# Delta rule's triangular matrices and their 32-block inverses issued beside the HGRN2 heads, and four PSUM banks for the levels

## The chip, the cores and the metric

One core of a Trainium2 chip runs one program: one layer of a diffusion backbone on 2048 latent and 128 context tokens. The metric is the device time of one execution in microseconds (us); the median of three runs counts. PE is TensorE (PEld its weight loads), DVE VectorE, ACT ScalarE, POOL GpSimd, SP the engine that issues this kernel's DMAs.

## The reference, cut to what matters

Two kinds of heads read one input projection. The first kind (HGRN2, "group A") is a gated linear recurrence over chunks of tokens, forward and backward. The second (gated DeltaNet, "group B") needs, per chunk, head and direction, the inverse of a unit lower triangular matrix that is made of keys and decays:

```
lower = where(strict, einsum('bhntk,bhnsk->bhnts', k_beta, k) * decay_mask, 0.0)
sol = triangular_solve(lower + eye(CHUNK), rhs, lower=True, unit_diagonal=True)
...
v_new = u_c - einsum('bhck,bhkv->bhcv', w_c, s)
o_c = einsum('bhtk,bhkv->bhtv', q_c, s) + einsum('bhts,bhsv->bhtv', attn_c, v_new)
s = s * d_c[..., None, None] + einsum('bhsk,bhsv->bhkv', kt_c, v_new)
```

The outputs of both kinds are normalised, gated, concatenated and projected; a SwiGLU feed-forward part follows.

## The kernel before

The kernel works on 17 chunks of 128 tokens (16 latent, one context), with 4 heads of each kind. Projections are cut into five pieces of 384 or 512 tokens; each piece is 24 matmuls (L257, tile `pj`, three PSUM banks), since weights and input are split in two parts for precision. In order:

- **Stage 1** (to about 494 us): norms, the delta rule's q, k, v columns and their convolution; the result goes to a DRAM scratch, `qkv_d`.
- **HGRN2 stage** (about 494 to 1040 us): per head a projection for q and one for v, then per direction one projection for the forget gate. The forget-gate pieces feed a chain: tanh and log on ACT (L488, L492), `th` on POOL (L494), a cumulative sum on DVE (L497 or L501), its middle subtracted on POOL (`G`, L508), two exponentials on ACT (L511, L512), two products on DVE (L515, L516), then small matmuls (L520 to L549). The state runs from chunk to chunk through three DVE operations, `T` (L547), `ns` (L552) and `ns` scaled (L553). "Gate half" below means the time of a head in which this chain runs; "value half" is the other, with the q and v projections.
- **Gate stage** (about 1040 to 1309 us): eight projections of output gates (`gate_block`, 960 matmuls on `pj`), and beside them the delta rule's matrices in three steps. `A1`, per chunk: keys loaded (`kTa`), four 128x128 products into a PSUM tile `pkk` (L592), decays per direction (`e`: a DMA broadcast, a mask on POOL at L599, an exponential on ACT at L602), the product of both on DVE (L604), a sum on POOL (L606) and a write to DRAM. `A2`, per batch of four chunks (one batch holds the context chunk alone): the 32x32 diagonal blocks come back into `A`, and a loop of 30 steps with two operations each (`pr`, L635, and `A`, L637) inverts them all at once. Three batches run on DVE, two on POOL. `A3`, per chunk ("levels"): 32-blocks are joined to 64 and 128 with small matmuls (tiles `pl` and `pn`, L675 to L701) and copies on ACT, POOL and DVE, from two PSUM banks and, for the later chunks, buffers that A1 no longer needs; the inverse goes to DRAM (`xt_d`).
- **Scan stage** (about 1309 to 1835 us): the delta rule's 16 steps in both directions, and the output projection's two halves as filler. Up to 1525 us the first half (`py`, L847) is under way; this is called the scan stage's first part.
- **Feed-forward stage** (from 1835 us).

Each engine takes its instructions in a fixed order, which a scheduler derives at build time from the order of the code, priorities and buffers; an instruction that waits holds everything behind it on its engine. All DMAs named here are issued by SP in one such order. `high_priority(1000)` lifts the A2 loops ahead of other work.

Of the kernel before, what the change touches and what calls it, by code (L numbers as in the profile page):

```python
# [24 lines left out]
H = 4  # L25
# [8 lines left out]
def hybrid_step(ctx: ExitStack, tc, x, vecs, ada1, ada2, bada, win, wgt, alog, dtb, sa, sb, wout, wg, wu, wd, normf,  # L34
# [37 lines left out]
    def tri(b, j, dims):  # L72
        return bass.AP(l_d[b].tensor, l_d[b].offset + j * 16 * BQ, dims)
# [64 lines left out]
        return (pl or gc).tile(shape, F32, tag=name, name=name)  # L138

    G, nG, eG, eL, ek, nrho, vbs, nrg = (K([P, 2, NT, H], n_) for n_ in "G nG eG eL ek nrho vbs nrg".split())  # L140
    gq = pool(sK, "gq", right=True)
    bp = pool(sB, "bp", right=True)
    gts = K([P, NT, 16], "gts", bp)
    pjp = pool(s1, "pjp", 3, PSUM, right=True)
# [293 lines left out]
                nc.vector.tensor_tensor(out=nrg[:, d], in0=nrho[:, d], in1=eG[:, d], op=ALU.mult)  # L438


    with ExitStack() as sA:
        ap_ = pool(sA, "ap", 1)
        smask = ap_.tile([P, 512], F32, tag="smask", name="smask")

        mki = []
# [10 lines left out]
        for h in range(H):  # L456
# [3 lines left out]
            for i, (c0, n) in enumerate(PIECES):  # L460
                pj = proj(w, i)
                th = ap_.tile([P, 512], F32, tag="th", name="th", bufs=2)
                nc.scalar.activation(out=th[:, :n * P], in_=pj, func=AF.Tanh, scale=0.5)
                nc.vector.scalar_tensor_tensor(out=q2[i], in0=th[:, :n * P], scalar=1.0, in1=pj, op0=ALU.add,  # L464
                                               op1=ALU.mult)
            w = load_w(win[12 + h])
            for i, (c0, n) in enumerate(PIECES):
                pj = proj(w, i)
                th = ap_.tile([P, 512], F32, tag="th", name="th", bufs=2)
                nc.scalar.activation(out=th[:, :n * P], in_=pj, func=AF.Copy)  # L470
                pt = ps1.tile([P, 4, P], F32, tag="tr", name="ptv", bufs=2)
                for j in range(n):
                    nc.tensor.transpose(pt[:, j, :], th[:, j * P:(j + 1) * P], ident)
                nc.scalar.activation(out=vt[i], in_=pt[:, :n], func=AF.Copy, scale=0.5)
            for d in range(2):
                col = d * H + h
                w = load_w(win[4 + 4 * d + h])
# [5 lines left out]
                for i in order:  # L483
# [75 lines left out]
                    else:  # L559
                        of = ap_.tile([P, 4, P], F32, tag="of", name="of", bufs=1)[:, :n]  # L560
                        dma(out=of, in_=oav[:, c0:c0 + n, h, :])
                        nc.vector.tensor_tensor(out=og, in0=po[:, :n], in1=of, op=ALU.add)
                    dma(out=oav[:, c0:c0 + n, h, :], in_=og)

    sp1.close()

    def bcast_G(t, d, c):
        dma(out=t.rearrange("p h t -> p (h t)"),
            in_=gr_d[d].rearrange("(c h) t -> c (h t)", h=H)[c:c + 1, :].broadcast_to([P, H * P]))

    def rep_h(m):
        return m.rearrange("p (a t) -> p a t", a=1).to_broadcast([P, H, P])

    s1b = ExitStack()
    count = [0, 0]
    psl = pool(s1b, "psl", 2, PSUM)
    psp = pool(s1b, "psp", 2, PSUM)


    with ExitStack() as sG:  # L580
        gp = pool(sG, "gp", right=True)

# [3 lines left out]
        def A1(c, b, j):

            kT = W([P, H, P], "kTa")
            dma(out=kT, in_=qkv_d[c, :, 0])
            pk = psp.tile([P, H, P], F32, tag="pre", name="pkk")  # L590
            for h in range(H):
                nc.tensor.matmul(out=pk[:, h], lhsT=kT[:, h], rhs=kT[:, h], start=True, stop=True)  # L592
            es = []
            for d in range(2):
                e = W([P, H, P], "e", 4)
                es.append(e)
                bcast_G(e, d, c)
                s = 1 if d == 0 else -1
                nc.gpsimd.affine_select(out=e, in_=e, pattern=[[0, H], [-s, P]], compare_op=ALU.is_gt, fill=1e30,  # L599
                                        base=0, channel_multiplier=s)  # L600
                for h in range(H):
                    nc.scalar.activation(out=e[:, h], in_=e[:, h], func=AF.Exp, scale=-1.0, bias=G[:, d, c, h:h + 1])  # L602
                for h in range(H):
                    nc.vector.scalar_tensor_tensor(out=e[:, h], in0=pk[:, h], scalar=nrho[:, d, c, h:h + 1],  # L604
                                                   in1=e[:, h], op0=ALU.mult, op1=ALU.mult)
            nc.gpsimd.tensor_tensor(out=es[0], in0=es[0], in1=es[1], op=ALU.add)  # L606
            dma(out=tri(b, j, [[P, P], [4 * BQ, H], [1, P]]), in_=es[0])

        def A2_load(b):

            nf = 16 * NB[b]
            pb = max(nf, 32)
            np_ = pb + nf
            A = W([P, 32, 32], "A", 2)
            B = W([P, 32, 32], "B")
            if nf < pb:
                nc.gpsimd.memset(A[0:pb], 0.0)
            for t, p0 in ((A, 0), (B, pb)):
                dma(out=t[p0:p0 + nf], in_=tri(b, 0, [[BQ, nf], [P, 32], [1, 32]]))
            nc.vector.tensor_copy(out=A[pb:np_], in_=B[pb:np_].rearrange("p a b -> p b a"))  # L620
            nc.gpsimd.affine_select(out=A[0:np_], in_=A[0:np_], pattern=[[1, 32], [-1, 32]], compare_op=ALU.is_gt,
                                    fill=0.0, base=0, channel_multiplier=0)
            nc.gpsimd.memset(A[0:np_].rearrange("p a b -> p (a b)")[:, 0:1024:33], 1.0)
            return A

        def A2(b, A, e=nc.vector):

            nf = 16 * NB[b]
            pb = max(nf, 32)
            np_ = pb + nf  # L630
            pr = W([P, 240], "pr")
            for r in range(1, 31):
                m = 31 - r
                pv = pr[0:np_, 0:m * r].rearrange("p (i c) -> p i c", c=r)
                e.tensor_tensor(out=pv, in0=A[0:np_, r + 1:, r:r + 1].to_broadcast([np_, m, r]),  # L635
                                in1=A[0:np_, r:r + 1, :r].to_broadcast([np_, m, r]), op=ALU.mult)
                e.tensor_tensor(out=A[0:np_, r + 1:, :r], in0=A[0:np_, r + 1:, :r], in1=pv, op=ALU.add)  # L637
            T = W([P, 32, 32], "B")
            e.tensor_copy(out=T[0:np_], in_=A[0:np_].rearrange("p a b -> p b a"))
            for d, p0 in ((0, 0), (1, pb)):  # L640
                for a in range(2):
                    dma(out=xi_d[b][:, a, d], in_=(A, T)[a ^ d][p0:p0 + nf].rearrange("p a b -> p (a b)"))


        XT = [W([P, 2, H, P], f"XT{i}") for i in range(2)]
        NS = [W([P, 2, H, 64], "NS")]
        for t in XT + NS:
            nc.gpsimd.memset(t, 0.0)

        def A3(c, b, j):  # L650

            n = count[0]
            count[0] += 1
            xt = XT[n % 2]
            second = n >= NB[1] and n % 2 == 1

            dd = W([P, 2, 2, H, 32], "e", 4) if second else W([P, 2, 2, H, 32], "dd", 2)
            dma(out=dd.rearrange("p a d h s -> p (a d h) s"),
                in_=xi_d[b][j].rearrange("a d (h q) (i s) -> (q i) (a d h) s", q=4, s=32))
            L = W([P, H, P], "e", 4) if second else W([P, H, P], "L", 2)  # L660
            dma(out=L, in_=tri(b, j, [[P, P], [4 * BQ, H], [1, P]]))
            if second and len(NS) < 2:
                NS.append(W([P, 2, H, 64], "kTa"))
                nc.gpsimd.memset(NS[1], 0.0)
            na, s6 = (NS[int(second)][:, i] for i in range(2))
            g = lambda q: slice(32 * q, 32 * q + 32)
            for q in range(4):
                nc.scalar.activation(out=xt[g(q), :, :, g(q)], in_=dd[g(q), 1], func=AF.Copy)
# [35 lines left out]
                nc.vector.tensor_copy(out=xt[f, d, :, s], in_=p6[f, 1])  # L704
            dma(out=xt_d[c], in_=xt)

        batches = [[NL], [0, 15, 1, 14], [2, 13, 3, 12], [4, 11, 5, 10], [6, 9, 7, 8]]
        order = (1, 2, 3, 4, 0)
        blocks = []
        def chain(t):  # L710
            with tc.high_priority(1000):
                A2(order[t], blocks[t], nc.gpsimd if t in (3, 4) else nc.vector)

        def levels(t):
            for j, c in enumerate(batches[order[t]]):
                A3(c, order[t], j)

        for t in range(5):
            for j, c in enumerate(batches[order[t]]):
                A1(c, order[t], j)  # L720
            blocks.append(A2_load(order[t]))
            if t:
                chain(t - 1)
            if t == 1:
                levels(0)
        chain(4)
        for t in range(1, 5):
            levels(t)
# [831 lines left out]
```

## Time and profile before

| | |
|---|---|
| median of 3 runs | 3355.38 us (3352.89 to 3359.86) |
| the profiled execution's own time | 3358.57 us |
| its span | 3356.9 us |
| PE busy | 3121.5 us, 93% |
| DVE busy | 2089.0 us, 62% |
| ACT busy | 1519.0 us, 45% |
| POOL busy | 1254.8 us, 37% |
| mean granted TensorE clock | 0.964 |

The span is the time from the first to the last instruction; the execution's own time lies 1.7 us above it. Busy time is the union of an engine's instructions. PE's busy share says that PE is rarely without an instruction, not that it runs at its peak: at the lower of its two clocks it is busy for longer with the same work. So a stage is read by three figures, its length, PE's busy time and the granted clock, and by who ended PE's waits in it.

### The profile page before, as it was taken

The numbers are of one execution on the slowest core, as the hardware profiler recorded it, in microseconds if no ns is written. First come the engines' busy times: TensorE is split into PE (matmuls) and PEld (weight loads), VectorE is DVE, ScalarE is ACT, GpSimd is POOL, SyncE is SP. The second block draws the span as 40 slices with busy tenths as digits, with TensorE's granted clock in tenths as the row PEclk, the third lists the DMA queues.
The fourth block names the chain that finished last, engine by engine and source line by source line (L and its number), as shares of the span: only waits on it lengthen the run. The fifth ranks groups of instructions, "written<-read, shape, count | busy, mean of one in ns | idle before, by whom it ended". The sixth has DMA issues, their size and how long they took to land. (4 is left out here: it accounts for less than half of the span.)

```text
span 3356.9 us, 51604 instructions
## 1 busy us (share of the span) xinstructions
PE 3121.5 (93%) x18550; PEld 2792.2 (83%) x18550; DVE 2089.0 (62%) x4016; ACT 1519.0 (45%) x3233; POOL 1254.8 (37%) x1228
## 2 busy tenths in 40 slices
PE   7899989999999799998897999999999999899998
PEld 4687779999998677877786888888899998799997
DVE  4667744474553764564666777778565677565667
ACT  6455435374464544663764555454422223422222
POOL 1100001021121337413566544554545553544446
PEclk8999999999999988999998999999999999999999
DMA  5235410111114667877784877898656766655564
GB/s 221 72 109 145 116 55 29 53 44 36 53 39 138 172 179 230 265 249 253 240 263 152 304 287 286 298 325 314 223 192 212 240 211 230 228 193 194 184 201 155
DMA packets 331009, 620.12 MB, mean 185 GB/s; under 512 B 77818, under 2 KB 177954, under 8 KB 324354
## 3 DMA queue, kind: packets, MB, share of 16 engines
q1 hardware_dynamic: 330754, 616.83, 56.0%
q8 instruction: 147, 2.41, 0.3%
q14 instruction: 108, 0.88, 0.1%
HBM read 435.22 MB, written 181.51 MB: 184 GB/s over the span
## 5 line engine op out<-in xcount | busy, mean ns | idle before, releaser
L257 PE MATMUL pj<-hh,wh 128*128 128x384 f32 (+2 forms) x1480 | 546.0, 369 | 12.9 <-DVE q L464 6.6
L257 PE MATMUL pj<-hl,wh 128*128 128x384 f32 (+2 forms) x1480 | 545.2, 368 | 0.3 <-POOL hl L231 0.3
L257 PE MATMUL pj<-hh,wl 128*128 128x384 f32 (+2 forms) x1480 | 545.3, 369 | 0.0
L257 PEld LDWEIGHTS pj<-hh,wh 128*128 128x128 f32 (+1 forms) x1480 | 280.4, 189 | 45.5 <-DVE q L464 6.8
L257 PEld LDWEIGHTS pj<-hl,wh 128*128 128x128 f32 (+1 forms) x1480 | 280.1, 189 | 29.9 <-issue 3.1
L257 PEld LDWEIGHTS pj<-hh,wl 128*128 128x128 f32 (+1 forms) x1480 | 280.1, 189 | 28.7 <-issue 3.3
L1476 POOL TENSOR_TENSOR u<-u,g 128x384 f32<-128x384 f32 (+1 forms) x132 | 136.3, 1033 | 292.7 <-DVE u L1217 242.8
L494 POOL TENSOR_SCALAR th<-th,nlbh,lbh 128x384 f32<-128x384 f32 (+1 forms) x40 | 60.5, 1513 | 405.8 <-ACT G L492 401.8
L1371 DVE TENSOR_TENSOR acc<-y,acc 128x512 f32<-128x512 f32 x192 | 131.7, 688 | 64.9 <-PE y L1367 58.0
L1209 PE MATMUL z<-x1h,wp 128*128 128x384 f32 (+1 forms) x528 | 142.8, 334 | 17.6 <-ACT wp L1067 14.2
L1067 ACT ACTIVATE wd<-wdr 128x512 fp32r<-128x512 f32 x146 | 90.0, 627 | 149.4 <-PE y L1367 95.4
L1367 PE MATMUL y<-wd,hid0h 128*128 128x512 f32 x432 | 136.4, 399 | 18.7 <-ACT hid0h L1067 10.0
L1464 ACT ACTIVATE g<-g 128x384 f32<-128x384 f32 (+1 forms) x132 | 66.7, 505 | 191.0 <-DVE g L1217 190.1
L1067 ACT ACTIVATE hid0h<-u 128x384 fp32r<-128x384 f32 (+3 forms) x113 | 53.3, 481 | 217.2 <-POOL u L1476 181.2
L1209 PE MATMUL z<-x6h,wp 128*128 128x384 f32 (+1 forms) x528 | 142.7, 333 | 7.2 <-ACT wp L1067 4.6
L246 DVE TENSOR_TENSOR wl<-raw,wh 128x512 fp32r<-128x512 f32 (+1 forms) x74 | 51.7, 698 | 153.6 <-ACT wh L245 153.5
L1371 DVE TENSOR_TENSOR sum<-y,sum 128x512 f32<-128x512 f32 x144 | 99.3, 690 | 75.8 <-PE y L1367 73.3
L1209 PE MATMUL z<-x4h,wp 128*128 128x384 f32 (+1 forms) x528 | 144.5, 331 | 1.3 <-DMA wp<-wpd 1.3
L1209 PE MATMUL z<-x7h,wp 128*128 128x384 f32 (+1 forms) x528 | 144.3, 332 | 1.0 <-DMA wp<-wpd 1.0
L1068 DVE TENSOR_TENSOR wd<-wdr,wd 128x512 fp32r<-128x512 f32 x146 | 111.9, 775 | 51.5 <-ACT wd L1067 50.6
L1209 PE MATMUL z<-x3h,wp 128*128 128x384 f32 (+1 forms) x528 | 142.6, 328 | 0.0
L1209 PE MATMUL z<-x2h,wp 128*128 128x384 f32 (+1 forms) x528 | 140.5, 328 | 1.4 <-DMA wp<-wpd 1.4
(414 smaller groups left out, 8850.6 us busy)
## 6 DMA issues: line engine op xcount, KB each, us to landing
wp<-wpd SPq DMA_DIRECT2D x308, 512.0 KB
wpd<-wp SPq DMA_DIRECT2D x154, 512.0 KB
ld<-qkvd SPq DMA_DIRECT2D x34, 1024.0 KB
wdr<-in_wd_dram SPq DMA_DIRECT2D x66, 512.0 KB
raw<-in_win_dram SPq DMA_DIRECT2D x72, 256.0 KB
e<-grd SPq DMA_DIRECT2D x68, 256.0 KB
at<-in_ada_dram SPq DMA_DIRECT2D x64, 256.0 KB
wr<-in_wg_dram SPq DMA_DIRECT2D x22, 512.0 KB
```

The costliest lines, as they stand in the source:

```text
L246: nc.vector.tensor_tensor(out=wl[:, ks], in0=raw, in1=wh[:, ks], op=ALU.subtract)
L257: nc.tensor.matmul(out=out, lhsT=a[:, k], rhs=b[:, k], start=t == 0, stop=t == 3 * KD - 1)
L494: nc.gpsimd.tensor_scalar(out=th, in0=th, scalar1=nlbh[:, col:col + 1], scalar2=lbh[:, col:col + 1], op0=ALU.mult, op1=ALU.add)
L1067: nc.scalar.activation(out=wh, in_=raw, func=AF.Copy)
L1068: (e or nc.vector).tensor_tensor(out=wl, in0=raw, in1=wh, op=ALU.subtract)
L1209: nc.tensor.matmul(out=z, lhsT=w_[:, k], rhs=x_[:, k, :N], start=t == 0, stop=t == 3 * HK - 1)
L1367: nc.tensor.matmul(out=py, lhsT=u_[:, j * P:j * P + P], rhs=v_, start=t == 0, stop=t == 2)
L1371: nc.vector.tensor_tensor(out=sums[i, j], in0=py, in1=sums[i, j], op=ALU.add)
L1464: nc.scalar.activation(out=g, in_=g, func=AF.Silu)
L1476: nc.gpsimd.tensor_tensor(out=us[i], in0=us[i], in1=gs[i], op=ALU.mult)
```

## The change

Lines of the changed kernel are higher by about 120 in the HGRN2 stage (L494 is L614, L508 is L628, L547 is L667) by 56 in the levels (L675 is L731), and by 37 behind the gate stage.

- A1 and A2 move from the gate stage to the HGRN2 stage, cut into steps. A1 is a load, `A1_decays` (mask and exponentials) and `A1` (matmuls, products, sum, write). A2 is six shares of five loop steps. A list of 65 steps is written out, and a function `beside`, called after each of the 80 pieces of the HGRN2 stage, issues as many steps as keep the list in even progress; it is empty four slots before the last.
- All five A2 batches run on POOL; no high priority is left.
- A1's product now lies in a bank of the pool that the transposes of the HGRN2 stage use (`tr`, two banks). Its buffers are single: one `kTa`, one `e` per direction, one `A`, `B` and `pr`, in a pool `ta` on the space that the gate tile `gct` had until then; `gct` is allocated anew in the gate stage.
- Levels get four PSUM banks in place of two, four `dd` and `L` buffers, three `XT` and two `NS` of their own; the loans of A1's buffers go.

```diff
+        ta = pool(sA, "ta", 1, right=True)
...
+        def A1_decays(c, b, j, kT, es):
+            for d in range(2):
...
+                nc.gpsimd.affine_select(out=e, in_=e, pattern=[[0, H], [-s, P]], compare_op=ALU.is_gt, fill=1e30,
+                                        base=0, channel_multiplier=s)
+                for h in range(H):
+                    nc.scalar.activation(out=e[:, h], in_=e[:, h], func=AF.Exp, scale=-1.0, bias=G[:, d, c, h:h + 1])
...
+            pk = ps1.tile([P, H, P], F32, tag="tr", name="pkk", bufs=2)
...
+        def A2(b, A, r0, r1):
+            e = nc.gpsimd
...
+            for r in range(r0, r1):
...
+        steps = [load_next] + chunk * 4
+        for n, b in enumerate(border):
+            mine = [lambda b=b, r=r: block(b, r, r + 5) for r in range(1, 31, 5)]
+            more = chunk * len(batches[border[n + 1]]) if n < 4 else []
+            while mine or more:
+                steps += [l.pop(0) for l in (mine, more) if l]
+        slots = [0, 5 * 4 * H]
+        def beside():
+            slots[0] += 1
+            while steps and len(steps) * (slots[1] - 8) > (slots[1] - 4 - slots[0]) * nsteps:
+                steps.pop(0)()
...
-    psl = pool(s1b, "psl", 2, PSUM)
-    psp = pool(s1b, "psp", 2, PSUM)
+    psl = pool(s1b, "psl", 4, PSUM)
...
-        XT = [W([P, 2, H, P], f"XT{i}") for i in range(2)]
-        NS = [W([P, 2, H, 64], "NS")]
+        XT = [W([P, 2, H, P], f"XT{i}") for i in range(3)]
+        NS = [W([P, 2, H, 64], f"NS{i}") for i in range(2)]
...
-            dd = W([P, 2, 2, H, 32], "e", 4) if second else W([P, 2, 2, H, 32], "dd", 2)
+            dd = W([P, 2, 2, H, 32], "dd", 4)
...
-            L = W([P, H, P], "e", 4) if second else W([P, H, P], "L", 2)
+            L = W([P, H, P], "L", 4)
...
-        def chain(t):
-            with tc.high_priority(1000):
-                A2(order[t], blocks[t], nc.gpsimd if t in (3, 4) else nc.vector)
...
+        for b in border:
+            for j, c in enumerate(batches[b]):
+                A3(c, b, j)
```

How instructions stand now, at three places. On POOL, in a gate half of the HGRN2 stage, before (`th` and `G` are the chain's two steps):

```order
L494 TENSOR_SCALAR th<-th,nlbh,lbh 128x512
L508 TENSOR_TENSOR G<-G,gm 128x512
L494 TENSOR_SCALAR th<-th,nlbh,lbh 128x384
L508 TENSOR_TENSOR G<-G,gm 128x384
L494 TENSOR_SCALAR th<-th,nlbh,lbh 128x384
```

and in the changed kernel, in the second head's gate half (`pr` and `A` are the A2 loop, `e` the sum of A1):

```order
L614 TENSOR_SCALAR th<-th,nlbh,lbh 128x384
L512 TENSOR_TENSOR pr<-A 128x210
L628 TENSOR_TENSOR G<-G,gm 128x384
L514 TENSOR_TENSOR A<-A,pr 128x21x10
L512 TENSOR_TENSOR pr<-A 128x220
L514 TENSOR_TENSOR A<-A,pr 128x20x11
L512 TENSOR_TENSOR pr<-A 128x228
L514 TENSOR_TENSOR A<-A,pr 128x19x12
L482 TENSOR_TENSOR e_5608<-e_5608,e_5609 128x512
L512 TENSOR_TENSOR pr<-A 128x234
L614 TENSOR_SCALAR th<-th,nlbh,lbh 128x384
```

Between two `th` of the chain now stand one `G` and eight operations that were not in this stage.

On DVE, in the first head's gate half, before (the cumulative sum into `G`, its middle `gm`, and the state's steps):

```order
L497 SCALAR_TENSOR_TENSOR G<-smask,G 128x384
L506 COPY gm<-G 128x3
L516 TENSOR_TENSOR e_4278<-e_4278,th 128x384
L552 TENSOR_TENSOR ns<-T,pu 128x128
L553 TENSOR_SCALAR ns<-ns,eg 128x128
L547 TENSOR_SCALAR T<-ns,eg 128x128
```

and in the changed kernel (the two rows of L480 are A1's products of one chunk, four heads each):

```order
L617 SCALAR_TENSOR_TENSOR G<-smask,G 128x384
L480 SCALAR_TENSOR_TENSOR e_4085<-pkk,nrho,e_4085 128x128 x4
L480 SCALAR_TENSOR_TENSOR e_4086<-pkk,nrho,e_4086 128x128 x4
L626 COPY gm<-G 128x3
L672 TENSOR_TENSOR ns<-T,pu 128x128
L673 TENSOR_SCALAR ns<-ns,eg 128x128
L667 TENSOR_SCALAR T<-ns,eg 128x128
```

A1's eight products stand between the cumulative sum and the copy of its middle, for which POOL's `G` waits, and ahead of the state's steps.

On DVE in the gate stage, before (A2's loop with A1's products and a weight split, `wl`, between its steps):

```order
L637 TENSOR_TENSOR A<-A,pr 128x27x4
L635 TENSOR_TENSOR pr<-A 128x130
L604 SCALAR_TENSOR_TENSOR e<-pkk,nrho,e 128x128
L637 TENSOR_TENSOR A<-A,pr 128x26x5
L604 SCALAR_TENSOR_TENSOR e<-pkk,nrho,e 128x128 x7
L635 TENSOR_TENSOR pr<-A 128x150
L246 TENSOR_TENSOR wl<-raw,wh 128x512
```

and at the start of the gate stage in the changed kernel (`og` is the HGRN2 stage's last output; the copies out of `pl` and `pn` are those of the levels):

```order
L682 TENSOR_TENSOR og<-po,of 128x512
L746 COPY XT_9652<-pl_9674 32x4x32 x2
L744 COPY NS_9655<-pn_9708 32x4x32
L746 COPY XT_9652<-pl_9674 32x4x32 x2
L247 TENSOR_TENSOR wl<-raw,wh 128x512
L744 COPY NS_9655<-pn_9708 32x4x32
L247 TENSOR_TENSOR wl<-raw,wh 128x512
L760 COPY XT_9652<-pl_9723 64x4x64 x2
```

The levels begin as soon as the HGRN2 stage ends, and DVE holds nothing but their copies and the weight splits in this stage.

## Rows read from the trace of the kernel before

**Rows 1.** Busy time by stage: length, PE, PEld, DVE, ACT, POOL, clock, DMA.

```profile
core 0: us, PE busy (x) PEld busy (x) DVE busy (x) ACT busy (x) POOL busy (x), PEclk, DMA share, GB/s
494.00:1040.00 546.00, 537.04 (x3256) 501.43 (x3257) 285.84 (x689) 281.18 (x440) 98.26 (x80) 0.99 0.14 42
1040.00:1309.00 269.00, 231.62 (x1937) 205.84 (x1936) 151.49 (x410) 132.50 (x274) 107.35 (x176) 0.92 0.65 180
1309.00:1525.00 216.00, 204.54 (x1868) 175.88 (x1868) 126.85 (x335) 136.30 (x412) 75.95 (x123) 0.94 0.80 262
```

**Rows 2.** PE's waits, HGRN2 stage (first two), then gate stage: us, times, longest.

```profile
PE pk L521 <- DVE e L516: 8.3, 4, 2.1
PE pj L257 <- DVE q L464: 6.6, 1, 6.6
...
PE pkk L592 <- DMA kTa<-qkvd: 30.1, 8, 11.5
```

**Rows 3.** Timeline, PE: one chunk's product of A1.

```profile
1055.62 1.05 PE L592 MATMUL pkk<-kTa 128*128 128x128 f32 x8
```

**Rows 4.** Busy time in the scan stage's first part, tiles pl, then pn.

```profile
1309.00:1525.00 216.00, 33.92 (x800) 30.25 (x799) 16.69 (x50) 5.30 (x17) 0.94 0.80 262
...
1309.00:1525.00 216.00, 7.56 (x136) 5.65 (x136) 4.88 (x18) 0.94 0.80 262
```

**Rows 5.** Groups of instructions on POOL, 1040 to 1525 us (busy us, mean ns).

```profile
L637 POOL TENSOR_TENSOR A<-A,pr 128x30 f32<-128x30 f32 (+29 forms) x60 | 31.7, 528 | 4.1
L635 POOL TENSOR_TENSOR pr<-A 128x30 f32<-128x30 f32 (+29 forms) x60 | 31.7, 528 | 6.0 <-DVE A L637 1.9
L606 POOL TENSOR_TENSOR e<-e 128x512 f32<-128x512 f32 x17 | 23.4, 1379 | 20.4 <-DVE e L604 16.9 <-DVE A L637 3.3
L599 POOL TENSOR_SCALAR_AFFINE_SELECT e<-e 128x512 f32<-128x512 f32 x34 | 23.0, 677 | 96.3 <-DMA e<-grd 96.2
```

**Rows 6.** Groups on DVE, then ACT, gate stage.

```profile
L604 DVE SCALAR_TENSOR_TENSOR e<-pkk,nrho,e 128x128 f32<-128x128 f32 x136 | 38.4, 342 | 36.5 <-PE pkk L592 26.3 <-ACT e L602 10.1
L635 DVE TENSOR_TENSOR pr<-A 128x30 f32<-128x30 f32 (+14 forms) x90 | 37.5, 417 | 4.9 <-POOL A L621 2.6
...
L602 ACT ACTIVATE e<-e,G 128x128 f32<-128x128 f32 x136 | 42.9, 390 | 45.7 <-POOL e L599 45.2
```

**Rows 7.** Groups on POOL, HGRN2 stage, with the idle time before them.

```profile
L494 POOL TENSOR_SCALAR th<-th,nlbh,lbh 128x384 f32<-128x384 f32 (+1 forms) x40 | 60.5, 1513 | 405.8 <-ACT G L492 401.8 <-issue 4.0
L508 POOL TENSOR_TENSOR G<-G,gm 128x384 f32<-128x384 f32 (+1 forms) x40 | 37.7, 943 | 11.1 <-DVE gm L506 10.6
```

**Rows 8.** Busy time as in rows 1: a gate half, then a value half.

```profile
690.00:710.00 20.00, 19.53 (x134) 19.49 (x135) 15.96 (x43) 15.90 (x25) 5.35 (x5) 1.00 0.17 53
...
770.00:801.00 31.00, 31.00 (x166) 28.09 (x165) 3.73 (x6) 7.31 (x14) 0.00 (x0) 1.00 0.11 35
```

**Rows 9.** Timeline of a gate half, DVE and POOL: start, duration.

```profile
711.02 0.77 DVE L547 TENSOR_SCALAR T<-ns,eg 128x128 f32<-128x128 f32 x1
...
712.54 0.29 DVE L547 TENSOR_SCALAR T<-ns,eg 128x128 f32<-128x128 f32 x1
...
710.88 0.83 POOL L508 TENSOR_TENSOR G<-G,gm 128x384 f32<-128x384 f32 x1 [0.17 <-DVE gm L506]
```

**Rows 10.** Groups on DVE, HGRN2 stage.

```profile
L547 DVE TENSOR_SCALAR T<-ns,eg 128x128 f32<-128x128 f32 x120 | 41.3, 344 | 24.1 <-PE po L549 19.3
L553 DVE TENSOR_SCALAR ns<-ns,eg 128x128 f32<-128x128 f32 x120 | 40.7, 339 | 3.0
...
L515 DVE TENSOR_TENSOR e<-e,q 128x384 f32<-128x384 f32 (+1 forms) x40 | 24.3, 608 | 0.9
L516 DVE TENSOR_TENSOR e<-e,th 128x384 f32<-128x384 f32 (+1 forms) x40 | 24.2, 604 | 8.4 <-ACT e L512 8.4
```

**Rows 11.** Busy time as in rows 1: scan stage, its start and a little later.

```profile
1310.00:1320.00 10.00, 7.60 (x78) 7.20 (x78) 7.59 (x21) 7.07 (x27) 5.05 (x10) 0.50 0.66 184
...
1330.00:1340.00 10.00, 10.00 (x127) 8.17 (x126) 5.03 (x8) 4.75 (x15) 7.05 (x11) 1.00 1.01 382
```

More of the change, by code (lines that the diff above doesn't have):

```diff
@@ L140, in hybrid_step @@
     G, nG, eG, eL, ek, nrho, vbs, nrg = (K([P, 2, NT, H], n_) for n_ in "G nG eG eL ek nrho vbs nrg".split())
-    gq = pool(sK, "gq", right=True)
+    sQ = ExitStack()
+    gq = pool(sQ, "gq", right=True)
     bp = pool(sB, "bp", right=True)
@@ L465, in hybrid_step @@
                                                op1=ALU.mult)
+                beside()
             w = load_w(win[12 + h])
@@ L474, in hybrid_step @@
                 nc.scalar.activation(out=vt[i], in_=pt[:, :n], func=AF.Copy, scale=0.5)
+                beside()
             for d in range(2):
@@ L563, in hybrid_step @@
                     dma(out=oav[:, c0:c0 + n, h, :], in_=og)
+                    beside()
+        assert not steps
     sp1.close()
-    def bcast_G(t, d, c):
-        dma(out=t.rearrange("p h t -> p (h t)"),
-            in_=gr_d[d].rearrange("(c h) t -> c (h t)", h=H)[c:c + 1, :].broadcast_to([P, H * P]))
     def rep_h(m):
@@ L575, in hybrid_step @@
     count = [0, 0]
-    psl = pool(s1b, "psl", 2, PSUM)
-    psp = pool(s1b, "psp", 2, PSUM)
+    psl = pool(s1b, "psl", 4, PSUM)
     with ExitStack() as sG:
+        gq = pool(sG, "gq", right=True)
         gp = pool(sG, "gp", right=True)
@@ L584, in W @@
             return gp.tile(shape, dt, tag=tag, name=tag, bufs=bufs)
[L586 to L642, printed above, removed]
@@ L653, in A3 @@
             count[0] += 1
-            xt = XT[n % 2]
-            second = n >= NB[1] and n % 2 == 1
-            dd = W([P, 2, 2, H, 32], "e", 4) if second else W([P, 2, 2, H, 32], "dd", 2)
+            xt = XT[n % 3]
+            dd = W([P, 2, 2, H, 32], "dd", 4)
             dma(out=dd.rearrange("p a d h s -> p (a d h) s"),
                 in_=xi_d[b][j].rearrange("a d (h q) (i s) -> (q i) (a d h) s", q=4, s=32))
-            L = W([P, H, P], "e", 4) if second else W([P, H, P], "L", 2)
+            L = W([P, H, P], "L", 4)
             dma(out=L, in_=tri(b, j, [[P, P], [4 * BQ, H], [1, P]]))
[L662 to L665, printed above, removed]
+            na, s6 = (NS[n % 2][:, i] for i in range(2))
             g = lambda q: slice(32 * q, 32 * q + 32)
@@ L705, in A3 @@
             dma(out=xt_d[c], in_=xt)
-        batches = [[NL], [0, 15, 1, 14], [2, 13, 3, 12], [4, 11, 5, 10], [6, 9, 7, 8]]
-        order = (1, 2, 3, 4, 0)
-        blocks = []
-        def chain(t):
-            with tc.high_priority(1000):
-                A2(order[t], blocks[t], nc.gpsimd if t in (3, 4) else nc.vector)
[L714 to L728, printed above, removed]
+        for b in border:
+            for j, c in enumerate(batches[b]):
+                A3(c, b, j)
         for b in range(8):
```

74 lines of the change are left out of this document (added).

## The prediction

> **What bounds the kernel now.** I read the busy time by stage first, since the change moves work from one stage to another. Three stages touch it [rows 1]. In the HGRN2 stage PE is busy for 537.0 of 546 us at a granted clock of 0.99: PE bounds it, and what it gets in addition makes it longer. In the gate stage PE is busy for 231.6 of 269 us at 0.92; 37.4 us are idle, and a clock of 0.92 means that 16% of the time, 43 us, ran at the lower of PE's two levels (1.2 in place of 2.4 GHz), where work takes twice as long: up to 21 us more. In the scan stage's first part PE is busy for 204.5 of 216 us at 0.94. So the gate stage is the loose one.
>
> Then PE's waits [rows 2]: 30.1 us of the gate stage's 37.4 idle us were ended by the arrival of A1's keys `kTa`. PE's order holds A1's product between projections, and a late key holds the projections behind it. In the HGRN2 stage there is hardly a wait, 14.9 us in all.
>
> Last, who has room. POOL in the HGRN2 stage waits 405.8 us for its next `th` [rows 7]; in a value half it does nothing [rows 8]. DVE is different: in a gate half it is busy for 15.96 of 20 us, in a value half for 3.73 of 31 [rows 8]. ACT has 15.90 of 20 in the same gate half.
>
> **The change, part by part.** The sum is made against the profiled execution's 3358.6 us, which lies 3.2 us above the median of the three runs; I take the same difference off the median.
>
> *1. A1's products in the HGRN2 stage.* A chunk's eight matmul records took 1.05 us [rows 3], 17 chunks 17.9 us. PE has 9 idle us in 546 [rows 1], so nothing hides them: +18.
>
> *2. New waits in the HGRN2 stage.* POOL gets 5 batches x 60 operations x 0.528 us = 158 us of A2, and from A1 17 x (1.379 + 2 x 0.677) = 46 us [rows 5]; with its own 98 it comes to some 300 of 546 us, so POOL does not bound. By POOL's order some 185 of the 300 A2 operations and about 9 of the 17 chunks stand in gate halves: 98 + 25 = 123 us in four gate halves of some 80 us, 38% of their time. DVE gets A1's products, 8 x 0.342 = 2.74 us a chunk [rows 6], 25 us in the gate halves. And DVE waits for POOL: a `T` that began while POOL's `G` ran took 0.77 us, another one 0.29 us, and it ended only after POOL's operation had [rows 9]. The operations of that sort on the chain, both inputs in SBUF, are 120 `T`, 120 scaled `ns` and 80 products [rows 10]; if 38% of these 320 meet an A2 operation and wait for half of its 0.528 us, that is 32 us. Together 57 us on DVE, against idle time of 4.04 in 20 us, 65 us in four gate halves. DVE would be nearly full there. PE feels what does not fit. Bounds: 0 (all of it falls into idle time) and +57 (none does); I take half of the waits, +16, since PE's few waits [rows 2] say that the chain runs well ahead of PE.
>
> ACT gets 136 exponentials of 0.390 us [rows 6], 53 us, of which 28 in gate halves with 66 idle us: nothing, as long as that idle time is there; without it they would add to term 2. SP issues 17 x 4 + 5 x 6 = 98 more DMAs in this stage. The DMA engines are busy for 0.14 of it [rows 1]; but SP's order puts weight loads behind writes that wait for POOL's sum. Weights have two buffers, so I count nothing, at worst some us. A late `e` also holds POOL's queue, and with it `th`; POOL's 405.8 idle us are the cover.
>
> *3. The gate stage.* From 269 us go A1's products, 18, and the waits for their keys, 30.1. The nine chunks of levels that ran after 1309 us come in: 33.9 + 7.6 = 41.5 us of PE time [rows 4]; the order sets each dependent group of a level some 20 projection matmuls behind the one it needs. A2's 75 us on DVE (90 pairs, one half of them in rows 6) and A1's POOL and ACT work leave, so copies come sooner. With PE fed without such waits I take the clock to cost 9 in place of 21 us, -12 (bounds 0 and -19, the HGRN2 stage's 0.99). 269 - 18 - 30.1 + 41.5 - 12 = 250: -19. This assumes that four banks keep up with 17 chunks in 250 us, 15 us a chunk. If the levels stayed at the old pace, their rest would move back into the scan stage, as now.
>
> *4. The scan stage's first part.* The same 41.5 us leave it. Not all is won: at its start, while the first loads land, levels were the filler, and even so PE was busy for only 7.6 of 10 us at 0.50 [rows 11]. I add 9 idle us there (bounds 4 and 20): -32.
>
> Sum: 18 + 16 - 19 - 32 = -17. From 3358.6 that is 3341.6 for the profiled execution, and **3338 us** for the median.
>
> **The rivals.**
>
> *A, slower: DVE and POOL get in each other's way in the gate halves.* For it: [rows 9], and DVE's 15.96 of 20 us [rows 8]. The place is the state's chain `T`, `ns`, scaled `ns`, on which each chunk's matmuls wait. It decides from the point where DVE's 57 added us no longer fit into its 65 idle us because they come in bunches: the second and the fourth head's gate halves hold a whole A2 batch each. Then term 2 is +57, and the sum +24: 3379. The Trainium skill (SBUF — State Buffer, "Who interferes with whom") says that a DVE operation with two SBUF inputs or in a 2-port mode and a GpSimd operation that reads SBUF share a port pair as an exclusive lock, held for a whole instruction. The trace agrees: 0.77 us against 0.29 [rows 9]. By that rule the two times add up rather than overlap, and the sum would be this rival's +24 instead of -17. Against it: PE waits only 14.9 us in this stage [rows 2], so there is depth in the chain.
>
> *B, no difference: the scan stage's first part is paced by its transfers.* From 1330 to 1340 us the DMA engines are busy for 1.01 of the time at 382 GB/s [rows 11]. If the loads of the scan set the pace, PE's 41.5 us turn into idle time but for what the levels' own transfers took of it; at a quarter, term 4 is -8 and the sum +7: 3362. Against it: at the same time PE is busy for all of the 10 us, and the share over the whole part is 0.80 [rows 1].
>
> *C, better: no new waits at all.* Term 2 is 0, the clock gives 19, the bubble costs 4: 18 - 26 - 37 = -45: 3310. For it: POOL's idle time, and a list that spreads its steps evenly.
>
> That the change does not do what it says is excluded by the order: all of A1 and A2 stands before the first level.
>
> **How the numbers follow.** My forecast gets 0.41 (3322 to 3350 by itself), C 0.24, A 0.22, B 0.13. Within 0.2% of the median, about what a measurement of this kernel can tell from no change, is 3348.7 to 3362.1. Faster: nearly all of the forecast and C, 0.63. Same: the forecast's upper edge, half of B and A's mild cases, 0.13. Slower: 0.24. The range goes from C's 3310, a little under it for a scan stage that gains its full 41.5, to near A's end: 3306 to 3376.
>
> **What would show it.** Right: the gate stage at about 250 us with no wait for `kTa`, a clock near 0.96 and all 17 chunks of levels inside; no `pl` behind its end; the HGRN2 stage at some 580 us, with `T` at a mean between 344 [rows 10] and some 450 ns. Wrong: an HGRN2 stage above 610 us, with PE waiting for `T` or for products of DVE (A); the scan stage's first part as long as before, with PE idle under full DMA engines (B); or levels still running beside the scan, which would say that four banks do not carry the pace.

## The result and the profile after

The change takes 3394.2 us (median of 4, 3391.41 to 3404.36) beside 3357.6 us of the kernel before on the same chip: a ratio of 1.012 (95%: 1.0103 to 1.0138), slower by some 37 us where 17 us of gain were forecast. The profiled execution took 3392.8 us, span 3391.1. Line numbers are those of the changed kernel: in the heads 120 more than before (`T` is L667).

The stages end later, so the answer to [rows 1] has other bounds: HGRN2 stage, gate stage, scan stage's first part (to the same `py` product).

```profile
494.00:1143.00 649.00, 581.16 (x3413) 535.62 (x3414) 361.53 (x835) 323.19 (x579) 320.38 (x449) 0.95 0.27 75
1143.00:1377.00 234.00, 234.00 (x2712) 206.45 (x2711) 50.00 (x147) 88.37 (x160) 23.14 (x73) 1.00 0.45 125
1377.00:1549.00 172.00, 150.91 (x842) 126.35 (x841) 93.66 (x249) 112.88 (x343) 32.75 (x36) 0.95 0.79 265
```

Against 546, 269 and 216 us: +103, -35, -44; the rest of the span is 10 us longer (1842 against 1832): the second half of `py` takes back 18 us of what its first half gained (328 against 310 us), and the feed-forward stage is 8 us shorter. Together +34, as the two spans differ. In the gate stage PE is never idle and at full clock, and all levels are in it; tile `pl`, gate stage and scan stage's first part, answers to [rows 4]:

```profile
1143.00:1377.00 234.00, 64.40 (x1632) 55.85 (x1632) 33.70 (x102) 10.89 (x34) 1.00 0.45 125
1377.00:1549.00 172.00, 0.00 (x0) 0.00 (x0) 0.00 (x0) 0.00 (x0) 0.95 0.79 265
```

The HGRN2 stage is the loss. PE is idle for 649 - 581 = 68 us, 59 more than before; A1's products are 18; the granted clock of 0.95 in place of 0.99 is 0.04 x 649 = 26 us of full-speed work. That makes 103. PE's busy time says the same: it rose by 44 us, of which 18 are the products. PE's longest waits there, against [rows 2]:

```profile
PE po L669 <- DVE T L667: 17.0, 10, 5.4
PE pk L641 <- DVE e L636: 16.0, 3, 11.5
PE pj L258 <- DVE q L582: 11.4, 1, 11.4
```

PE waits for DVE, but DVE waits in turn. One stall shows the chain, read backwards. In the timeline of the change, PE, DVE, ACT, POOL and SP between 643 and 671 us (start, duration, instruction, idle time before it and what ended it):

```profile
670.30 0.79 PE L669 MATMUL po<-T,e 128*128 128x128 f32 x2 [5.25 <-DVE T L667]
...
668.78 0.55 DVE L582 SCALAR_TENSOR_TENSOR q<-th,pj 128x384 f32<-128x384 f32 x1 [7.85 <-ACT th L581]
...
663.96 1.28 ACT L470 ACTIVATE e<-e,G 128x128 f32<-128x128 f32 x4 [16.43 <-POOL e L467]
...
668.28 0.47 ACT L581 ACTIVATE th<-pj 128x384 f32<-128x384 f32 x1
...
663.29 0.64 POOL L467 TENSOR_SCALAR_AFFINE_SELECT e<-e 128x512 f32<-128x512 f32 x1 [16.67 <-DMA e<-grd]
...
643.23 1.20 SPq L521 DMA_DIRECT2D xid<-A  x2
644.53 2.13 SPq L456 DMA_DIRECT2D kTa<-qkvd  x1
646.70 1.54 SPq L521 DMA_DIRECT2D xid<-B  x1
648.36 1.31 SPq L683 DMA_DIRECT2D oad<-og  x1
649.71 1.93 SPq L681 DMA_DIRECT2D of<-oad  x1
651.67 2.15 SPq L521 DMA_DIRECT2D xid<-B  x1
653.87 2.23 SPq L483 DMA_DIRECT2D ld<-e  x1
656.21 6.68 SPq L444 DMA_DIRECT2D e<-grd  x2
```

At 643 us POOL's elimination of a batch ends, and SP, which had stood 7.5 us at the first write of its inverses, issues the four writes (`xid`, 256 KB each). In its order they stand ahead of A1's write (`ld`) and of the loads of the next decays `e`. SP's issues from 644 to 656 us (`oad` and `of` are the heads' outputs) take 1.3 to 2.2 us each. POOL's sum, which A1's write carries, ended at 646.6; the write was issued at 653.9 and the first load of `e` at 656.2, and this load landed at 663. (The row of 6.68 us joins two loads. The longest issue of an `e` load in the trace is 1.84 us; the second load waited 4.4 us until A1's write, which reads its tile, had landed.) Until then POOL stands at its mask, ACT at the exponential behind the mask, with the next `th` of the q projection behind it, and DVE at `q`, with the next `ns` and `T` behind it. PE gets its `T` at 670.3. POOL's groups in the stage, and SP's waits (us in total, times, longest):

```profile
L514 POOL TENSOR_TENSOR A<-A,pr 128x30 f32<-128x30 f32 (+19 forms) x150 | 88.3, 588 | 9.9
L512 POOL TENSOR_TENSOR pr<-A 128x30 f32<-128x30 f32 (+19 forms) x150 | 82.9, 553 | 9.4
L614 POOL TENSOR_SCALAR th<-th,nlbh,lbh 128x384 f32<-128x384 f32 (+1 forms) x40 | 49.2, 1229 | 64.6 <-ACT G L612 64.6
L467 POOL TENSOR_SCALAR_AFFINE_SELECT e<-e 128x512 f32<-128x512 f32 x34 | 22.6, 665 | 211.1 <-DMA e<-grd 211.1
```

```profile
SPq L456 <- PE pkk L476: 59.9, 6, 22.4
SPq L521 <- POOL A L514: 52.8, 5, 19.5
SPq L483 <- POOL e L482: 48.2, 12, 10.2
SPq L444 <- DMA ld<-e: 31.4, 16, 7.6
```

POOL's 405.8 idle us ahead of `th` [rows 7] have become 64.6 there and 211.1 at A1's mask (125.4 of them a single wait that ends as the stage begins; in the kernel before POOL idles there as long, so 85.7 us are the stage's own). DVE's `T` has a mean of 403 ns (344 before, [rows 10]).

### The profile page after: what moved, and what is told of

Same layout as the page of the kernel before. It is cut to its first block, busy times and chain, and to the rows that moved or that the text cites. A ratio compares the mean times of both kernels' runs of the same rounds, so it can differ in the third digit from the quotient of the medians.

```text
span 3391.1 us, 51630 instructions
## 1 busy us (share of the span) xinstructions
PE 3121.9 (92%) x18550; PEld 2786.1 (82%) x18550; DVE 2042.3 (60%) x3833; ACT 1504.1 (44%) x3223; POOL 1354.8 (40%) x1412
## 4 chain that ended last, share of the span: by engine, by line
PE 48%; DMA 14%; DVE 13%; POOL 10%; ACT 9%; issue 6%; SPq 1%; POOLq 0%; DVEq 0%; ACTq 0%
PE z L1246 18%; PE pj L258 11%; PE y L1404 7%; DMA e<-grd 2%; PE py L884 2%; POOL A L514 2%; POOL pr L512 2%; DMA wdr<-in_wd_dram 2%; PE y L1443 2%; DMA at<-in_ada_dram 2%; DVE ct L354 1%; DMA o<-oad 1%; DMA raw<-in_win_dram 1%; DVE acc L296 1%; DVE wp L1105 1%
## 5 line engine op out<-in xcount | busy, mean ns | idle before, releaser
L1246 PE MATMUL z<-x5h,wp 128*128 128x384 f32 (+1 forms) x528 | 142.6, 334 | 0.5 <-DMA wp<-wpd 0.4
L1254 DVE TENSOR_TENSOR u<-z,u 128x384 f32<-128x384 f32 (+1 forms) x165 | 84.9, 531 | 91.6 <-PE z L1246 90.8
```

Of the source, the lines that this page charges most:

```text
L1246: nc.tensor.matmul(out=z, lhsT=w_[:, k], rhs=x_[:, k, :N], start=t == 0, stop=t == 3 * HK - 1)
L1254: nc.vector.tensor_tensor(out=out, in0=z, in1=b, op=ALU.add)
```

## The experiments

"Stage" in this table is the HGRN2 stage from 494 us to the end of the last product `po<-T`; PE idle is its length less PE's busy time; ratios are to the kernel before on the same chip, with 95% intervals. The runs come from several chips, on which the kernel before took 3348.9 to 3357.6 us; so differences between runs are taken below from the ratios, times 3355 us.

| run | us | ratio | stage | PE idle | `T`, ns |
|---|---|---|---|---|---|
| before | 3348.9 to 3357.6 | 1 | 544 | 9 | 344 |
| the change | 3394.2 | 1.0120 (1.0103-1.0138) | 648 | 68 | 403 |
| e1_spread | 3394.7 | 1.0131 (1.0109-1.0153) | 643 | 68 | 432 |
| e2_no_elimination | 3337.0 | 0.9951 (0.9933-0.9970) | 589 | 30 | 331 |
| e3_two_banks | 3391.8 | 1.0115 (1.0091-1.0139) | 646 | 65 | 400 |
| e4_value_halves | 3396.7 | 1.0138 (1.0111-1.0164) | 646 | 75 | 386 |
| e5_a2_in_gate_stage | 3378.9 | 1.0084 (1.0061-1.0107) | 579 | 28 | 314 |
| e6_split | 3386.1 | 1.0107 (1.0086-1.0128) | 603 | 44 | 332 |
| e7_before_plus_pool | 3362.9 | 1.0039 (1.0024-1.0054) | 553 | 17 | 395 |
| e8_writes_from_pool | 3375.6 | 1.0071 (1.0047-1.0095) | 628 | 59 | 413 |
| e9_elimination_detached | 3362.0 | 1.0030 (1.0014-1.0046) | 612 | 42 | 416 |
| e10_transfers_from_pool | 3362.9 | 1.0042 (1.0027-1.0057) | 622 | 47 | 456 |
| e11_elimination_on_dve | 3373.4 | 1.0066 (1.0049-1.0083) | 631 | 55 | 335 |
| e12_combined | 3376.5 | 1.0082 (1.0065-1.0099) | 629 | 58 | 469 |
| e13_pool_transfers_no_elim | 3332.2 | 0.9942 (0.9929-0.9954) | 583 | 27 | 352 |
| e14_copy_on_pool | 3359.5 | 1.0024 (1.0011-1.0036) | 609 | 43 | 494 |
| e15_one_batch_beside | 3363.9 | 1.0031 (1.0021-1.0041) | 588 | 27 | 355 |
| e16_two_batches_beside | 3351.5 | 0.9997 (0.9983-1.0011) | 595 | 29 | 424 |

### Late transfers, POOL's work, or the banks

**e1_spread.** A1's and A2's steps at fixed slots, loads ahead:

```diff
-            while steps and len(steps) * (slots[1] - 8) > (slots[1] - 4 - slots[0]) * nsteps:
-                steps.pop(0)()
+            for f in plan.pop(slots[0], ()):
+                f()
```

> The steps at fixed slots: a chunk's three loads, two slots later its mask and exponentials, one slot later its products, and the next loads only then; a batch's loads one slot or more ahead of what reads them. Nothing is added or left out. Theory H (in the HGRN2 stage the in-order queues of POOL, ACT and DVE are held by late transfers of the steps, and PE idles behind them): POOL's idle time ahead of the mask falls from 211 us to under 80, PE's idle time in the stage from 68 us to under 35, and with it the stage from 649 us to under 615; the time is 3350 to 3368 us. Theory K (POOL and DVE lengthen each other's instructions): the same instructions meet as often, the product for T keeps its mean of about 403 ns, and the time is within 8 us of 3394.

The time did not fall. The mask's row, POOL's groups in the stage:

```profile
L467 POOL TENSOR_SCALAR_AFFINE_SELECT e<-e 128x512 f32<-128x512 f32 x33 | 20.9, 635 | 90.7 <-DMA e<-grd 90.6
```

These 90.7 us stand against the change's 85.7, since the one long wait ahead of the stage ends at 493 us here and is not in the row (the longest in it is 15.0 us): the mask's waits within the stage did not fall. SP stood 81.8 us at A1's writes, 48.2 in the change. So the edit did not take the late transfers away, and the run is no test of H. PE is idle for the same 68 us, now mostly in front of `T` (34.3 us). The time is the one that K gave, though `T`'s mean rose to 432 ns where K had it stay.

**e2_no_elimination.**

```diff
-            for r in range(r0, r1):
+            for r in ():
```

> The change without the elimination of the 32-blocks: the 300 products and sums on POOL (171 us busy) are left out and the blocks' inverses are identities; loads, copies, masks and writes stay. Theory K: the mean for T goes from 403 to under 355 ns, DVE's busy time falls by 20 us or more, the HGRN2 stage by 30 us or more, the time to 3365 us or less. Theory H: the transfers and the waits for them stay, POOL still idles over 150 us ahead of the mask, the stage loses only what SP waited for the elimination: 5 to 20 us, the time 3374 to 3389 us.

3337.0 us: 57 us hang on the elimination, all in this stage.

```profile
494.00:1083.00 589.00, 559.10 (x3383) 518.86 (x3383) 335.29 (x833) 318.20 (x575) 160.44 (x149) 0.98 0.29 80
```

`T` fell to 331 ns, and stage and time fell as K said. The mask still waits 197.9 us, 124.6 of them the wait ahead of the stage. The run takes away two things, POOL's 171 us and the time for which the writes of the inverses wait.

**e3_two_banks.**

```diff
-    psl = pool(s1b, "psl", 4, PSUM)
+    psl = pool(s1b, "psl", 2, PSUM)
```

> The change with two PSUM banks for the levels in place of four, nothing else. If the banks made the gate stage shorter (269 to 222 us) and let all levels end ahead of the scan: the gate stage is 240 us or more, and the time 3405 to 3430 us. If what made it shorter is that the triangular matrices and inverses are gone from it: the gate stage stays under 230 us, and the time is within 8 us of 3394.

No difference that can be measured (3391.8), as the second branch said. With two banks some levels run beside the scan; tile `pl` in the gate stage and behind it:

```profile
1140.00:1360.00 220.00, 49.06 (x1254) 43.10 (x1255) 24.94 (x76) 8.40 (x26) 1.00 0.45 125
1360.00:1549.00 189.00, 19.79 (x388) 17.73 (x383) 8.81 (x26) 2.69 (x9) 0.92 0.75 254
```

The two together are 409 us, as long as the change's 234 + 172 = 406. What shortened the gate stage is that A1 and A2 are gone from it.

### DVE and POOL beside each other

**e7_before_plus_pool** puts POOL's work alone into the kernel before:

```diff
+                nc.gpsimd.tensor_copy(out=xp_[0:1, 0:1], in_=t)
+                for r in range(r0, r0 + 5):
...
+                    nc.gpsimd.tensor_tensor(out=xa[:, r + 1:, :r], in0=xa[:, r + 1:, :r], in1=pv, op=ALU.add)
```

> The kernel before with 30 groups of ten POOL products and sums on a tile of zeros that nobody reads, of the elimination's shapes on 128 partitions, each tied to the slot where the change has its step; no transfers, no waits of others on them. Theory K: the mean for T goes from 344 to 380 ns or more, the HGRN2 stage from 546 to 570 us or more, the time to 3380 to 3410 us. Theory H: POOL's idle time covers them, the stage grows by under 12 us, the time is under 3368 us.

`T` got as slow as in the change (DVE's group):

```profile
L569 DVE TENSOR_SCALAR T<-ns,eg 128x128 f32<-128x128 f32 x120 | 47.4, 395 | 20.3 <-PE po L571 14.9
```

```profile
494.00:1047.00 553.00, 536.16 (x3249) 497.73 (x3250) 308.64 (x693) 281.12 (x440) 268.25 (x413) 0.99 0.14 42
```

but the stage grew by 9 us and the time by 13, as H said. So the collisions are real and their price, on the kernel before, is a quarter of the elimination's 57. Over the table `T`'s mean does not go with the time: 494 ns at 3359 us, 335 at 3373.

**e4_value_halves** and **e6_split** tie elimination steps to value halves; e4 all of them, e6 two batches, the others in the gate stage on POOL:

```diff
+            nc.gpsimd.tensor_copy(out=pr[0:1, 0:1], in_=pin[0])
```

> All work as in the change, but each of the 30 elimination steps is tied by a one-element copy to a product of a value half (q, v projections) of the last three heads, where no chain of T and ns runs; A1's steps come every third slot. Theory K (the elimination on POOL beside the gate halves slows DVE's chain, and PE with it): the mean for T falls from 403 to under 380 ns, the HGRN2 stage from 649 to under 630 us, the time to 3350 to 3376 us. Theory H (late transfers hold the queues): transfers and waits are as many, the time is within 10 us of 3394.

> A1 beside the HGRN2 heads; two of the five batches are eliminated in value halves of the last two heads (tied there), three in the gate stage on POOL. Theory K: the HGRN2 stage 605 to 620 us, the gate stage at most 235 us, the time 3340 to 3370 us, within 10 us of the kernel with all of A2 in the gate stage. Theory H: 3385 us or more.

In both the time is H's and not K's. In e4 a large part of the elimination still ran in gate halves (between 719 and 762 us, for one), and `T`'s mean is 386 ns where K asked for less than 380, so it is a weak test of K; and it moves no write off SP. In e6 the stage is about what K said, 603 us, but the gate stage, with three batches' elimination on POOL in it, takes 269 us in place of 234.

**e5_a2_in_gate_stage:**

```diff
+        for b, e in zip(border, (nc.vector, nc.gpsimd, nc.vector, nc.gpsimd, nc.vector)):
+            A2(b, A2_load(b, W, (2,)), 1, 31, W, e)
```

> A1 stays beside the HGRN2 heads, A2 whole (loads, masks, elimination, writes) goes back to the gate stage, on DVE and POOL in turn; the levels keep four banks. Theory K: the HGRN2 stage falls from 649 to 600 us or less, as without the elimination or shorter, the gate stage grows from 222 to at most 250 us, the time is 3335 to 3365 us. Theory H: A1's loads and masks still hold POOL, the stage stays over 625 us, the time 3385 us or more.

The HGRN2 stage is 579 us, less than K asked for, but the inverses come later, the levels run on beside the scan, and the time, 3378.9, missed both ranges. Tile `pl`, gate stage and behind it:

```profile
1073.00:1336.00 263.00, 48.03 (x1152) 41.78 (x1152) 23.79 (x72) 7.72 (x24) 0.91 0.53 142
1336.00:1500.00 164.00, 24.70 (x480) 21.73 (x480) 9.91 (x30) 3.25 (x10) 0.90 0.73 231
```

### SP's order

**e9_elimination_detached** has POOL's work, but its writes do not wait for their own elimination (inverses are identities, as in e2):

```diff
+            if r0 == 1:
+                T = V([P, 32, 32], "B")
...
-                e.tensor_tensor(out=A[0:np_, r + 1:, :r], in0=A[0:np_, r + 1:, :r], in1=pv, op=ALU.add)
+                e.tensor_tensor(out=pv, in0=A[0:np_, r + 1:, :r], in1=pv, op=ALU.add)
```

> As the run without elimination (identities as the blocks' inverses, 3337 us), but POOL does 300 products and sums of the elimination's shapes at the same slots, reading the blocks and writing only the scratch tile; copies and writes of the inverses are issued ahead of them, so that no write waits for them. The elimination itself is left out. Theory Q: only the collisions come back, as on the kernel before (13 us): the stage 589 to 605 us, the time 3340 to 3360 us. Theory P: the stage is over 630 us, the time over 3380 us, as in the change.

3362.0 is 2 us above Q's range and far below P's; the stage, 612 us, is 7 above Q's. By the ratios the elimination's 57 us are 27 for the work (1.0030 against 0.9951) and 30 for the writes that wait for it (1.0120 against 1.0030), each give or take 8. So the work costs twice what e7 showed. SP still stood at the writes, behind the copy ahead of them on POOL, but for less than the change's 52.8 us:

```profile
SPq L514 <- POOL pr L518: 21.6, 6, 6.1
```

**e8_writes_from_pool:**

```diff
-            dma(out=tri(b, j, [[P, P], [4 * BQ, H], [1, P]]), in_=es[0])
+            nc.gpsimd.dma_start(out=tri(b, j, [[P, P], [4 * BQ, H], [1, P]]), in_=es[0])
...
-                    dma(out=xi_d[b][:, a, d], in_=(A, T)[a ^ d][p0:p0 + nf].rearrange("p a b -> p (a b)"))
+                    nc.gpsimd.dma_start(out=xi_d[b][:, a, d], in_=(A, T)[a ^ d][p0:p0 + nf].rearrange("p a b -> p (a b)"))
```

> The change, with the writes of A1 (a chunk's triangle) and of A2 (the inverses) issued on POOL's own queue, behind the sum or the elimination that they wait for, and no longer on SP's. Theory Q (SP's in-order queue stands at a write until POOL's elimination or sum is done, 52.8 and 48.2 us, with the weights' loads, A1's loads and the outputs' writes and reads behind it): the HGRN2 stage falls from 648 to under 615 us and the time to 3345 to 3372 us. Theory P (POOL's queue itself is what is late: masks, sums, th and G behind the elimination): the stage stays over 630 us, the time over 3380 us, since POOL has more to do.

3375.6, between the two: 16 us saved although POOL has 37 issues more. SP then stood at the loads of `e` (61.6 us behind POOL's sum).

**e10_transfers_from_pool** moves these too, and sums into the tile of `kTa` so that `e` is free at once:

```diff
-                bcast_G(es[d], d, c)
+                bcast_G(es[d], d, c, nc.gpsimd.dma_start)
...
-            nc.gpsimd.tensor_tensor(out=es[0], in0=es[0], in1=es[1], op=ALU.add)
+            nc.gpsimd.tensor_tensor(out=kT, in0=es[0], in1=es[1], op=ALU.add)
```

> The change, with all transfers of A1 and the writes of A2 issued on POOL's queue; the sum goes to the tile of the chunk's k in place of a decay tile, so that the next decays are loaded without waiting for the write, and k is loaded behind the masks. SP keeps A2's reads alone. Theory Q (what remains over the run without elimination is SP standing at A1's loads and writes: kTa behind PE, up to 22 us each, e behind POOL): the HGRN2 stage falls from 628 us (writes alone moved) to under 612 us, the time from 3376 to 3345 to 3366 us. Theory P (POOL is late by its own work and its waits for the decays): the stage stays over 620 us, the time 3370 us or more.

```profile
L615 POOL TENSOR_SCALAR th<-th,nlbh,lbh 128x384 f32<-128x384 f32 (+1 forms) x40 | 47.5, 1187 | 52.0 <-ACT G L613 46.4 <-DVE ns L674 5.2
L465 POOL TENSOR_SCALAR_AFFINE_SELECT e<-e 128x512 f32<-128x512 f32 x34 | 22.9, 682 | 21.9 <-DMA e<-grd 21.6
```

POOL's waits at the mask, 85.7 us in the change without the one ahead of the stage, are 21.9 us, and the time is 3362.9, about as in e9. The engines do the change's work, in 26 us less (give or take 8), by the transfers' queue and order and the sum's tile. The time fits Q. The stage, 622 us, is by 2 us in P's range, and not in Q's.

**e13_pool_transfers_no_elim** asked for the rest:

> As the run with all transfers of A1 and the writes of A2 on POOL's queue (3363 us, stage 622), with the elimination left out (identities as the blocks' inverses), as in the run without elimination (3337 us, stage 589). If SP standing at A1's loads and writes makes up the open 28 us: the stage falls to 575 us or less, the time to 3310 to 3326 us. If it is the steps' own work on ACT, DVE and POOL: the stage is 583 to 600 us, the time 3330 to 3345 us.

583 us and 3332.2, as the second branch said: 3 us less than e2 by the ratios, whose intervals overlap. So without the elimination no cost of SP's order can be measured. The stage is 39 us longer than in the kernel before: 18 are A1's products, 18 more idle time of PE. That these come from the steps' own work on ACT, DVE and POOL is what is left, not shown.

### Versions meant to be faster

**e11_elimination_on_dve**, **e12_combined** and **e14_copy_on_pool** start from e10 (e11: the loop on DVE, tied to value halves; e12: on POOL, tied, first chunk later, `kTa` ahead of the masks; e14: the copy behind A2's reads on POOL):

> As the run before (all transfers but A2's reads from POOL), A1's steps every third slot, and the 300 products and sums of the elimination on DVE, tied to products of the value halves of the last three heads (about 0.35 us each by the gate stage of the kernel before, 105 us, against 171 us on POOL). Theory P: POOL is free for masks, sums, th and G, T's mean falls under 360 ns, the HGRN2 stage under 605 us, the time to 3335 to 3360 us. If DVE, which runs the chain of T and ns, is the worse place: the stage is over 625 us and the time over 3375 us.

> As the run with all transfers of A1 and the writes of A2 on POOL's queue (3363 us), with three more edits: the first chunk's decays are tied to the fourth q product, so that the stage's first masks and q products do not stand behind them (there PE idled 10 us); k is loaded ahead of the masks, not behind; and the elimination, on POOL, is tied to the value halves of the last three heads. By theories P and Q together: the stage falls from 622 to 590 to 606 us, PE's idle time from 47 to under 30 us, the time to 3333 to 3350 us, below the kernel before (3351). If the value halves' place is worth nothing, as it was while the transfers were SP's, only the start is saved: 3350 to 3358 us.

> As the run with the transfers from POOL (3363 us), with the five transposing copies behind A2's reads on POOL in place of DVE, so that DVE no longer waits for those reads (19 us in 4 waits there). If these waits hold PE: the stage falls from 622 to under 612 us, the time to 3343 to 3356 us. If not, or if POOL's waiting is as bad: within 6 us of 3363.

e11 and e12 missed. In e11 `T` came to 335 ns as said, but the stage is 631 us, as if DVE were the worse place. In e12 the next order took over; DVE's longest wait in the stage:

```profile
DVE A L510 <- DMA B<-ld: 63.5, 5, 25.0
```

DVE, with the state's chain behind, stood at the copy for A2's reads, which SP held until the last batch's writes had landed. e14 takes this wait off DVE; the stage fell to 609 us as forecast, but the time's interval overlaps e10's, so it settles nothing.

**e15_one_batch_beside** and **e16_two_batches_beside** (from e14: one or two batches on POOL beside the heads, the others on DVE in the gate stage):

```diff
+        late = [(b, A2_load(b, W, (4,))) for b in border[2:]]
+        for n, b in enumerate(border):
+            if n >= 2:
+                A2(*late.pop(0), 1, 31, W, nc.vector, dma)
```

> From the run with transfers and copies on POOL (3359 us, HGRN2 stage 609 to 622): only the first batch is eliminated beside the heads; the loads of the other four come at the start of the gate stage, each on tiles of its own, and their 240 products and sums go to DVE there, between the levels. If the cost belongs to the place: the HGRN2 stage falls to 585 to 598 us, the gate stage (258 us to the first py) grows by at most 12, the time is 3330 to 3346 us. If it comes back as a wait of the levels: levels run on beside the scan, the gate stage or the scan grows by 20 us or more, the time is 3352 us or more.

> The same with two batches eliminated beside the heads and three on DVE in the gate stage. If the cost belongs to the place: the HGRN2 stage is 590 to 605 us, the gate stage as long as in the change, the time 3335 to 3350 us. If it comes back as a wait of the levels: 3352 us or more.

e16 is 41 us faster than the change and as fast as the kernel before (0.9997); its 3351.5 us fall between its two ranges. The HGRN2 stage and the gate stage are

```profile
494.00:1089.00 595.00, 565.78 (x3403) 525.15 (x3404) 338.30 (x830) 324.00 (x578) 258.18 (x334) 0.97 0.26 75
1089.00:1344.00 255.00, 243.11 (x2722) 214.78 (x2721) 116.28 (x331) 89.27 (x160) 36.95 (x83) 0.97 0.50 133
```

From the HGRN2 stage's end to the first `py` product pass 275 us, 248 in the change. With one batch (e15) the HGRN2 stage is 588 us as forecast, but then 290 us pass, and the time is in the second range: the cost comes back behind the stage. No version that does all the work beat the kernel before.

## Why the prediction was wrong

- **Term 1, A1's products (+18):** right; 17 chunks at the price of [rows 3], in the open.
- **Term 2, new waits in the HGRN2 stage (+16, bounds 0 and +57):** this step failed. It measured +85 (103 less the 18 of term 1), beyond its upper bound. By the stage lengths these are about 27 for the steps without the elimination (e2), 23 for the elimination's work (e9 over e2) and 36 for the writes that wait for it (the change over e9). The bounds were worked out for DVE's and POOL's collisions alone, and +16 was about right in size for those: 13 us by e7, 27 by e9 and e2. Two sentences that priced the rest at nothing were wrong. "I count nothing, at worst some us" for SP: a write in SP's order that waits for a slow engine holds the loads behind it, 30 us by e9 and 26 by e10. "POOL's 405.8 idle us are the cover": a sum of idle time did not cover a single wait of 16.7 us, because whoever waits for POOL has others behind it in turn. ACT's exponentials, priced at nothing too, were one link of that chain: in the stall shown ACT stood 16.4 us at them, with the next `th` of the q projection behind. And I gave the stage no change of clock; 26 of the 85 us are PE at its lower level after the stalls.
- **Term 3, the gate stage (-19):** right in direction, too small: -35. No wait for `kTa`, clock 1.00; I had kept 9 us of clock loss and 7 of idle time. That four banks carry the pace came true, but nothing hung on it: with two, a quarter of the `pl` matmuls ran on beside the scan, as the prediction had it for a slow pace, and the time was the same (e3).
- **Term 4, the scan stage's first part (-32):** -44 in this part, with no level left in it, of which 10 came back behind it: -34. Terms 3 and 4 together gave -69 where -51 was forecast, so the total hides 18 us of what term 2 missed.
- **Rivals:** A had the direction, and what it named as its mark came (stage above 610 us, PE waiting for `T` and DVE's products), but its mechanism is only a part of the cause: 13 us on the kernel before (e7), 27 by e9 and e2, where the rival had 57. B and C did not come about.
- **Open:** what makes up the 18 us of PE's idle time in e13, and why the elimination's work costs 27 us by e9 and 13 by e7. No run leaves the writes on SP and only moves them behind the loads, or moves them to a queue other than POOL's; so the waiting at a write and the slow issues that follow it are not told apart.

## What to carry to other kernels

Before work is put "beside" a stage, follow each of its transfers through the queue that issues it: a write that waits for a slow engine belongs in that engine's own queue, behind its producer, and not ahead of the loads of the main chain. Do not take an in-order engine's summed idle time as cover: compare the longest single wait with the time by which the chain runs ahead. Then price a stall of PE for the clock as well: here 59 us more of idle time came with 26 us of PE's work at its lower level.

## What the runs showed of the hardware

A stall of a few microseconds costs more than its length. Around the one at 665 us (the change, busy time and granted clock as in [rows 1]):

```profile
665.00:670.00 5.00, 0.06 (x1) 0.00 (x0) 1.07 (x4) 2.79 (x8) 0.63 (x1) 0.98 0.32 95
670.00:672.00 2.00, 1.70 (x6) 1.60 (x7) 1.82 (x6) 0.00 (x0) 0.00 (x0) 0.50 0.00 0
672.00:674.00 2.00, 2.00 (x8) 1.68 (x8) 1.04 (x2) 0.00 (x0) 0.00 (x0) 0.70 0.51 124
674.00:676.00 2.00, 2.00 (x10) 1.65 (x10) 0.69 (x1) 0.80 (x2) 0.00 (x0) 1.00 0.47 138
```

PE was idle for 5.25 us, and the clock was at 0.50, its lower level of 1.2 GHz, when work came back, and at 1.00 again some 3 us later.

An issue on SP is not always short. Shortest, median and longest issue in ns, for a load of `e` and for A1's write in the change, then for the same write issued from POOL in e8:

```profile
L444 SPq DMA_DIRECT2D e<-grd x68: 319/330/1837, 490.5 to 1786.8; - x68
L483 SPq DMA_DIRECT2D ld<-e x17: 360/371/2230, 530.1 to 988.9; - x17
L483 POOL DMA_DIRECT2D ld<-e x17: 769/798/1002, 529.3 to 980.4; - x17
```

The longest two are those behind the burst of writes at 643 us. A transfer issued from POOL takes POOL's own time, 0.80 us for A1's write at the median.
